# Moving the reloads of the turned queries, and the joins that follow them, through the cross-attention stage of a decoder layer

## The chip, the cores and the metric

The kernel runs on one core of a Trainium2 chip. The metric is the device time of one execution in microseconds (us); lower is better. The kernel before was run three times: 1977.21, 1982.29 and 1982.72 us, median 1982.29 us. The execution that was profiled took 1977.05 us.

## The reference

One decoder layer on 256 tokens of width 2048 in float32: two token mixers side by side (retention and a gated linear recurrence), then cross-attention over 256 memory tokens, then a gated feed-forward block, each added to the residual stream. The change lies in the cross-attention:

```python
q = (hn @ w_q).reshape(b, s, 4, 512)
k = (mem_n @ w_k).reshape(b, m, 4, 512)
v = (mem_n @ w_v).reshape(b, m, 4, 512)
logits = einsum("bshd,bmhd->bhsm", q, k) * 512 ** -0.5
p = softmax(logits, axis=-1)
o = einsum("bhsm,bmhd->bshd", p, v)
h = h + o.reshape(b, s, 2048) @ w_o
```

There are four heads of 512 columns, so head b is the b-th block of 512 columns of q, k and v, and there are four softmaxes.

## The kernel before

**Units.** Every weight matrix is streamed from HBM in pieces of 512 rows by 512 columns (1 MB, tile `raw`, six buffers, L257). ScalarE (ACT) rounds a piece to `hi` (L288) and VectorE (DVE) takes the rest, `lo` (L289); each has three buffers. TensorE (PE) multiplies the activations with both. One piece, split and multiplied, is a unit. A matrix product over two column blocks is a pair of 11 units (`PAIR_UNITS`, L105): seven of them, the q units, issue 12 matmuls, and four, the p units, issue 24. In order they are q1 p0 q3 p1 q5 q2 q6 p2 q7 q4 p3. Two of the q units use a sum of pieces that GpSimd's accumulating DMA makes (`raw` from L269), and DVE adds pieces together once more behind q5 and q6 (L294, L296).

**What orders the work.** `units` (L310) hands out the pieces. Before unit n is multiplied it splits pieces up to unit n+2 (`prefetch`, L250), and after unit n it calls what `later(m, f)` (L306) has put down for that unit; `later(m, f)` means "after m more units than the next one". So what is called after unit n stands in the program behind `hi` and `lo` of unit n+2 and ahead of those of unit n+3. A scheduler then lays the instructions of each engine into one fixed queue in the order in which a simulation finds them ready, earlier program lines first; `keep_in_program_order` holds an instruction behind everything that the program gave its engine earlier. Each engine works through its queue in order, and waits where an input is not there.

**The stage.** The units are counted here from the start of the key product: units 0 to 10 are the first key pair (heads 0 and 1), 11 to 21 the second key pair (heads 2 and 3), 22 to 32 the value pair (heads 0 and 1 of the value), and from 33 on come the single value blocks of 24 matmuls each.

The queries come out of the preceding product with tokens on the partitions. They are wanted with features on the partitions, so they are turned by DMA, which moves two-byte words only: `row_planes` (L771, copies at L760) separates the high and the low halves of the words, `KeptRows.store` (L794) puts them to HBM, `KeptRows.load` (L801) reads one head back with a transposing DMA on the queue of SyncE (SP) into a tile `d`. `join_planes` (L762) puts the halves of a pair of feature blocks together again with two copies on ACT (L766, the first of them held in program order), and `split_pair` (L551) makes the two parts for the matmul: a cast on ACT (L555) and a subtraction on DVE (L556). That chain for one pair of blocks is called a join here. Each head has one reload and two joins. The keys take the same way without HBM: `turn_key` (L1244) turns a key block by two transposing DMAs from SBUF (`turn_planes`, L777, issued at L781), calls its two joins 6 and 7 units later, and the softmax of the head 9 units later. `softmax` (L1196) issues 24 small matmuls (L521, the first held in program order), the maximum, the exponential and the division, and two units later four transposes of the probabilities on PE (L1222, the first held in program order).

| called after unit | head 0 | head 1 | head 2 | head 3 |
|---|---|---|---|---|
| reload of the query, before | 2 | 6 | 14 | 19 |
| joins of the query, before | 6, 8 | 10, 12 | 18, 20 | 23, 25 |
| turn of the key | 12 | 16 | 23 | 27 |
| joins of the key | 18, 19 | 22, 23 | 29, 30 | 33, 34 |
| softmax | 21 | 25 | 32 | 36 |

Where a join of a query and one of a key are called after the same unit, that of the query comes first, since it was put down earlier. `d`, the joined and split tiles and the block outputs share one pool of 24 tiles of 4 KB per partition (`big`).

Of the kernel before, what the change touches and what calls it, by code (L numbers as in the profile page):

```python
# [156 lines left out]
def hybrid_layer(  # L157
# [148 lines left out]
    def later(n, fn):  # L306

        pending.append((step[0] + n + 1, fn))
# [139 lines left out]
    def pair_out(w, st, ss, c0, r=None):  # L448

        o0, o1 = (big([P, 2, BW], s="o") for _ in range(2))  # L450
        if r is not None:
            neg = sp_.tile([P, 2], F32, tag="neg", name=nm("neg"))
            dve.tensor_scalar_mul(neg, r, -1.0)

        def copy(o, i, tt):
            if r is None:
                act.copy(o, i)
            else:
                act.mul(o, i, r[:, tt : tt + 1])

        def add(o, i):
            if r is None:
                dve.tensor_tensor(out=o, in0=o, in1=i, op=ALU.add)
            else:
                for tt in range(2):
                    dve.scalar_tensor_tensor(
                        out=o[:, tt, :], in0=i[:, tt, :], scalar=r[:, tt : tt + 1], in1=o[:, tt, :],
                        op0=ALU.mult, op1=ALU.add,
                    )

        def less(o, i, tt):
            if r is None:
                dve.tensor_tensor(out=o, in0=o, in1=i, op=ALU.subtract)
            else:
                dve.scalar_tensor_tensor(
                    out=o, in0=i, scalar=neg[:, tt : tt + 1], in1=o, op0=ALU.mult, op1=ALU.add
                )

        def out(kind, x, z, yu, rw):
            if kind == "q1":  # L480
                copy(o0[:, 0, :], x, 0)
            elif kind == "q5":
                for tt in range(2):
                    copy(o1[:, tt, :], z, tt)
                later(3, lambda: add(o1, rw))
            elif kind == "q6":
                less(o1[:, 0, :], x, 0)
            elif kind == "q7":
                copy(o0[:, 1, :], x, 1)
                less(o1[:, 1, :], x, 1)  # L490
            elif kind == "p3":
                add(o0, yu)

        pair_products(w, 0, st, ss, c0, c0 + BW, out)
        return o0, o1
# [748 lines left out]
    def turn_key(b, o):  # L1244
        d = turn_planes(row_planes(o))
        ks = []
        for pr in range(2):
            later(5 + pr, lambda pr=pr: ks.append(split_pair(join_planes(d, pr))))
        later(8, lambda: softmax([qs[2 * b], qs[2 * b + 1]], ks))

    for b, at in ((0, ((2, 6, 8), (6, 10, 12))), (2, ((3, 7, 9), (8, 12, 14)))):
        for i, (n, *joins) in enumerate(at):
            later(n, qs.load)
            for pr, m in enumerate(joins):
                later(m, lambda i=2 * b + 2 * i + pr: qs[i])
        for i, o in enumerate(pair_out("xa_w_k", ms, ms.sums, b * BW, rsms[0])):
            later(1 + 4 * i, lambda b=b + i, o=o: turn_key(b, o))
# [229 lines left out]
```

## Time and profile before

| | |
|---|---|
| time of the profiled execution | 1977.05 us |
| its span, first to last instruction | 1975.3 us |
| mean granted TensorE clock | 0.999 |
| ACT busy in the span | 1295.6 us (66%) |
| DVE busy in the span | 1564.9 us (79%) |
| moved by DMA | 461.29 MB, mean 234 GB/s |

Times within the profile are microseconds from the start of the span. In a row of the timeline the first two numbers are the start and the length of an instruction (or of a run of equal ones, merged, with their count at the end); then come the engine, the line, the operation, and the tile written and the tiles read; the bracket has the idle time of the engine just before and what ended it. In a row of the groups the numbers behind the bar are the busy time and the mean time of one in ns, and behind the second bar the idle time before. PE is the matmul, PEld the load of its weights, which lies beside it. SPq rows are DMAs that SP issues: the length is that of the issue, not of the transfer.

### The profile page before, as it was taken

The page shows a single profiled execution, that of the slowest core. Times are in us where ns is not written, and L with a number is a line of the kernel's source. Part 1 is how long each engine was busy: PE and PEld are TensorE (multiplying, and loading weights), DVE is VectorE, ACT ScalarE, POOL GpSimd, SP SyncE. Part 2 cuts the span into 40 slices and gives each one's busy share as a digit, 9 for nine tenths or more (in the row PEclk, how much of TensorE's full clock was granted, in tenths as well). Part 3 has the DMA queues.
Part 4 walks back from the last instruction along what each step waited for, and adds up shares of the span by engine and source line. Part 5 has one row for each costly group of instructions (what it writes and reads, how often), then busy time and mean ns, then how long its engine had stood idle before and what let it go on. Part 6 is the DMA issues. An engine that isn't in the chain of part 4 may idle for free. (4 is left out here: it accounts for less than half of the span.)

```text
span 1975.3 us, 23603 instructions
## 1 busy us (share of the span) xinstructions
PE 1961.2 (99%) x9264; PEld 1645.0 (83%) x9264; DVE 1564.9 (79%) x1546; ACT 1295.6 (66%) x1349; POOL 43.2 (2%) x52
## 2 busy tenths in 40 slices
PE   9999999999999999999999999999999999999998
PEld 8888888888888888888888888888888888888887
DVE  6988887889986886778888868777779676796775
ACT  6655656767667656667778767666765577655663
POOL 0000000000000000000000000000000000000000
PEclk9999999999999999999999999999999999999999
DMA  9675774655887776878998838867689677797671
GB/s 369 232 253 147 244 254 172 214 194 158 259 257 240 255 236 212 245 288 239 280 262 224 284 128 250 274 220 212 222 224 305 234 230 225 204 302 271 215 244 63
DMA packets 157598, 461.29 MB, mean 234 GB/s; under 512 B 88368, under 2 KB 93104, under 8 KB 109744
## 3 DMA queue, kind: packets, MB, share of 16 engines
q1 hardware_dynamic: 150208, 415.23, 60.0%
q0 software_dynamic: 5760, 41.95, 11.5%
q10 hardware_dynamic: 1520, 2.63, 0.4%
q8 instruction: 72, 1.18, 0.2%
q14 instruction: 38, 0.31, 0.0%
HBM read 422.01 MB, written 17.83 MB: 223 GB/s over the span
## 5 line engine op out<-in xcount | busy, mean ns | idle before, releaser
L289 DVE TENSOR_TENSOR lo<-raw,hi 128x2048 fp32r<-128x2048 f32 (+1 forms) x420 | 950.8, 2268 | 290.6 <-ACT hi L288 288.6
L288 ACT CAST hi<-raw 128x2048 fp32r<-128x2048 f32 (+1 forms) x418 | 792.2, 1901 | 479.7 <-PE acc L365 311.6
L364 PE MATMUL acc<-hi,s 128*128 128x512 f32 x2008 | 783.1, 390 | 0.4 <-ACT hi L288 0.2
L365 PE MATMUL acc<-hi,s 128*128 128x512 f32 x2008 | 781.6, 389 | 0.0
L371 PE MATMUL acc<-lo,s 128*128 128x512 f32 x2008 | 500.7, 389 | 0.0
L364 PEld LDWEIGHTS acc<-hi,s 128*128 128x128 f32 x2008 | 376.9, 188 | 78.4 <-ACT hi L288 0.6
L371 PEld LDWEIGHTS acc<-lo,s 128*128 128x128 f32 x2008 | 376.9, 188 | 78.3
L365 PEld LDWEIGHTS acc<-hi,s 128*128 128x128 f32 x2008 | 377.1, 188 | 77.6 <-DVE s L559 0.2
L353 PE MATMUL acc<-s,hi 128*128 128x512 f32 x832 | 201.9, 394 | 1.1 <-DVE hi L286 1.1
L353 PEld LDWEIGHTS acc<-s,hi 128*128 128x128 f32 x832 | 154.3, 189 | 31.8 <-issue 1.4
L766 ACT COPY jp<-d 128x512 uint16<-128x512 uint16 x152 | 108.4, 772 | 33.1 <-DMA d<-rp 33.1
L364 PE MATMUL acc<-hi,ss 128*128 128x512 f32 x320 | 125.9, 394 | 2.3 <-DVE nat L429 1.5
L365 PE MATMUL acc<-hi,ss 128*128 128x512 f32 x320 | 124.7, 390 | 0.0
L353 PEld LDWEIGHTS acc<-s,lo 128*128 128x128 f32 x832 | 108.0, 192 | 4.7 <-DVE lo L289 1.0
L353 PE MATMUL acc<-s,lo 128*128 128x256 f32 x832 | 111.1, 284 | 0.4 <-DVE lo L289 0.4
L371 PE MATMUL acc<-lo,ss 128*128 128x512 f32 x320 | 85.9, 390 | 0.0
L364 PEld LDWEIGHTS acc<-hi,ss 128*128 128x128 f32 x320 | 60.1, 188 | 17.4 <-DVE nat L429 3.0
L371 PEld LDWEIGHTS acc<-lo,ss 128*128 128x128 f32 x320 | 60.1, 188 | 12.6
L365 PEld LDWEIGHTS acc<-hi,ss 128*128 128x128 f32 x320 | 60.1, 188 | 12.1
L269 POOL DMA_DIRECT2D raw<-in_wall x40 | 35.2, 880 | 1555.6 <-DVE lo L289 925.1
L429 DVE TENSOR_TENSOR nat<-nat,acc 128x512 f32<-128x512 f32 (+1 forms) x49 | 44.0, 910 | 3.4 <-DMA nat<-in_x 1.7
L294 DVE TENSOR_TENSOR raw<-raw,raw 128x2048 f32<-128x2048 f32 x20 | 45.8, 2288 | 0.5
(232 smaller groups left out, 1249.1 us busy)
## 6 DMA issues: line engine op xcount, KB each, us to landing
raw<-in_wall SPq DMA_DIRECT2D x333, 1024.0 KB, 5.0
raw<-in_wall POOLq DMA_DIRECT2D x40, 1024.0 KB, 8.2
fkept<-nat SPq DMA_DIRECT2D x12, 512.0 KB, 8.0
nat<-fkept SPq DMA_DIRECT2D x12, 512.0 KB, 4.8
xt<-in_x_t SPq DMA_DIRECT2D x11, 256.0 KB, 7.8
raw<-in_wall SPq DMA_DIRECT2D x5, 512.0 KB, 8.2
nat<-in_x ACTq DMA_DIRECT2D x4, 512.0 KB, 9.8
ret<-hr SPq DMA_DIRECT2D x4, 512.0 KB, 4.8
```

Of the source, the lines that this page charges most:

```text
L269: pool.dma_start(out=raw, in_=src, accum_op=ALU.add)
L288: act.copy(hi[:, a:b], raw[:, a:b])
L289: dve.tensor_tensor(out=lo[:, a:b], in0=raw[:, a:b], in1=hi[:, a:b].bitcast(F32), op=ALU.subtract)
L294: dve.tensor_tensor(out=to, in0=to, in1=by, op=ALU.add)
L353: pe.matmul(a, part, sx, start=k == 0 and t == 0, stop=k == nk - 1 and t == 0, skip_group_check=True)
L364: pe.matmul(o, h, hi, start=start and kk == 0, stop=False, skip_group_check=True)
L365: pe.matmul(o, l, hi, start=False, stop=False, skip_group_check=True)
L371: pe.matmul(o, h, lo, start=False, stop=stop and kk == KC - 1, skip_group_check=True)
L429: dve.tensor_tensor(out=o, in0=o, in1=i, op=op)
L766: ins = act.copy(words(t)[:, :, :, 1 - i], d[:, i, 2 * pr : 2 * pr + 2, :])
```

## The change

The two lists of offsets in the loop over the key pairs are replaced. Each inner list is the unit, from the start of its key pair, after which a head's query is reloaded, and the two units after which it is joined.

```diff
-    for b, at in ((0, ((2, 6, 8), (6, 10, 12))), (2, ((3, 7, 9), (8, 12, 14)))):
+    for b, at in ((0, ((3, 14, 15), (8, 18, 19))), (2, ((8, 12, 13), (14, 19, 20)))):
         for i, (n, *joins) in enumerate(at):
             later(n, qs.load)
             for pr, m in enumerate(joins):
                 later(m, lambda i=2 * b + 2 * i + pr: qs[i])
```

In units counted from the start of the first key pair:

| | head 0 | head 1 | head 2 | head 3 |
|---|---|---|---|---|
| reload, before | 2 | 6 | 14 | 19 |
| reload, after the change | 3 | 8 | 19 | 25 |
| joins, before | 6, 8 | 10, 12 | 18, 20 | 23, 25 |
| joins, after the change | 14, 15 | 18, 19 | 23, 24 | 30, 31 |

The turns of the keys, their joins, the softmaxes and all else are called where they were.

## The prediction

> **What bounds the kernel now.** The page comes first: the span, and the busy line of its engines.
>
> ```profile
> span 1975.3 us, 23603 instructions
> PE 1961.2 (99%) x9264; PEld 1645.0 (83%) x9264; DVE 1564.9 (79%) x1546; ACT 1295.6 (66%) x1349; POOL 43.2 (2%) x52
> ```
>
> TensorE is busy for 1961.2 of 1975.3 us. All that any change of order can win is the other 14.1 us, and only the part that lies in the stretch which the change touches. So the next view is the busy time in three stretches: the first key pair (units 0 to 10), the second (11 to 21, with the softmax behind it), and the value pair (22 to 32, with two softmaxes).
>
> ```profile
> core 0: us, PE busy (x) PEld busy (x) DVE busy (x) ACT busy (x) POOL busy (x), PEclk, DMA share, GB/s
> 978.60:1019.40 40.80, 40.80 (x182) 33.80 (x181) 36.67 (x26) 32.12 (x30) 1.74 (x2) 1.00 0.96 284
> 1019.40:1063.10 43.70, 43.70 (x206) 36.70 (x205) 38.24 (x27) 35.70 (x34) 1.74 (x2) 1.00 0.97 261
> 1063.10:1111.70 48.60, 47.70 (x238) 40.16 (x237) 40.23 (x34) 40.16 (x47) 0.88 (x1) 1.00 0.81 250
> ```
>
> In both key pairs PE is busy for the whole stretch; in the value pair it lacks 0.9 us. A busy PE could still be a slow one, so the third view is PE in order of time, at the place of that gap.
>
> ```profile
> 1089.60 0.39 PE L364 MATMUL acc<-hi,ss 128*128 128x512 f32 x1
> 1089.83 0.39 PE L365 MATMUL acc<-hi,ss 128*128 128x512 f32 x1
> 1090.05 0.84 PE L371 MATMUL acc<-lo,ss 128*128 128x512 f32 x3
> 1091.80 0.30 PE L1222 MATMUL sm<-cid,prob 128*128 128x128 f32 x1 [0.90 <-DVE prob L1215]
> ```
>
> Starts lie 0.23 us apart although each row is 0.39 us long: the matmuls overlap in the array, and that is the pace throughout (182 of them in the 40.80 us of the first stretch, 0.224 us each). Three of them from 1090.05 would be followed by a fourth at 1090.73; what follows starts at 1091.80. The one stall is thus 1.07 us (0.90 us of it shows as idle time): the transposes of the probabilities of head 1 wait for DVE. By rows this is the ceiling of the gain, and the question is only what new wait arises.
>
> **The change, part by part.** Nothing is added or removed. Eight joins and four reloads are called at other units. By the places where they are called, the query joins of the first key pair go from 3 to 0, those of the second from 3 to 4, those of the value pair from 2 to 4. A join costs two copies and a cast on ACT and a subtraction on DVE:
>
> ```profile
> L766 ACT COPY jp<-d 128x512 uint16<-128x512 uint16 x28 | 20.4, 780 | 0.0
> L555 ACT CAST s<-jp 128x512 fp32r<-128x512 f32 x14 | 8.7, 619 | 0.0
> L556 DVE TENSOR_TENSOR s<-jp,s 128x512 fp32r<-128x512 f32 x14 | 9.6, 686 | 2.1 <-ACT s L555 2.0
> ```
>
> That is 2 x 0.78 + 0.62 = 2.2 us of ACT and 0.7 us of DVE. The second key pair takes one join more: ACT 35.70 + 2.2 = 37.9 of 43.70 us, DVE 38.24 + 0.7 = 38.9. The value pair takes two more: ACT 40.16 + 4.4 = 44.6 of 48.60, DVE 40.23 + 1.4 = 41.6. Both engines still fit, so the averages cost PE nothing. The first pair gains 6.6 us of ACT, which is worth nothing, since PE already runs there without a gap.
>
> Averages can hide a bunch, so the margin of a single unit is needed. This is ACT in order of time, and PE where it takes up what the second of these `hi` casts made (unit 18):
>
> ```profile
> 1034.10 1.92 ACT L288 CAST hi<-raw 128x2048 fp32r<-128x2048 f32 x1 [2.62 <-PE acc L365]
> 1035.92 0.77 ACT L766 COPY jp<-d 128x512 uint16<-128x512 uint16 x1
> 1037.77 1.92 ACT L288 CAST hi<-raw 128x2048 fp32r<-128x2048 f32 x1 [1.08 <-issue]
> ```
> ```profile
> 1043.87 0.39 PE L364 MATMUL acc<-hi,s 128*128 128x512 f32 x1
> ```
>
> The cast ends at 1039.69, 4.2 us before PE needs it, and that is with ACT running as far ahead as three buffers let it (at 1034.10 it waits for PE). Joins 0 and 1 of head 0 are now called after units 14 and 15, that is about these two casts; the idle 2.62 and 1.08 us take most of their 4.4 us. The largest bunch is after units 18, 19, 23 and 30, where a query join stands beside a key join; 18 and 23 were such places before. At 19 and 30 the addition is 2.2 us, at 24 and 31 likewise, against 4.2 us of margin. I cost all delays of `hi` and `lo` at 0. If the margin were gone, each join would cost up to 2.2 us of PE.
>
> What is left are the waits of PE for a softmax, whose matmuls keep their place in PE's queue. There are three.
>
> Softmax of head 0, after unit 21. Here are ACT and DVE ahead of it, and PE:
>
> ```profile
> 1055.27 0.61 ACT L555 CAST s<-jp 128x512 fp32r<-128x512 f32 x1
> 1055.78 0.77 ACT L766 COPY jp<-d 128x512 uint16<-128x512 uint16 x1
> 1056.42 1.90 ACT L288 CAST hi<-raw 128x2048 fp32r<-128x2048 f32 x1
> 1058.22 0.62 ACT L555 CAST s<-jp 128x512 fp32r<-128x512 f32 x1
> ```
> ```profile
> 1057.01 0.69 DVE L556 TENSOR_TENSOR s<-jp,s 128x512 fp32r<-128x512 f32 x1
> 1058.36 2.29 DVE L289 TENSOR_TENSOR lo<-raw,hi 128x2048 fp32r<-128x2048 f32 x1 [0.66 <-ACT hi L288]
> 1060.57 0.69 DVE L556 TENSOR_TENSOR s<-jp,s 128x512 fp32r<-128x512 f32 x1
> ```
> ```profile
> 1060.19 3.04 PE L521 MATMUL sm<-s,s 128*128 128x256 f32 x24
> ```
>
> By program order the join cast at 1055.27 is the key's second (called after 19), and that at 1058.22 belongs to the query of head 2 (after 20). In the changed kernel the query of head 1 joins after 19 ahead of the key, and nothing is called after 20: the key moves to the later place, and its subtraction ends at 1061.26. The 24 matmuls take 0.12 us each, and the seventh, at 1060.91, is the first to read it. Cost 0.35 us.
>
> The stall ahead of the transposes of head 1. DVE before it:
>
> ```profile
> 1085.43 0.69 DVE L556 TENSOR_TENSOR s<-jp,s 128x512 fp32r<-128x512 f32 x1
> 1086.03 0.68 DVE L1205 TENSOR_REDUCE sx<-sm 128x2 f32<-128x512 f32 x1
> ...
> 1091.29 0.62 DVE L1215 TENSOR_SCALAR prob<-prob,sx 128x256 f32<-128x256 f32 x2
> ```
>
> The subtraction at 1085.43 is that of the last join, called after 25. It goes to 31, so the chain behind it can start 0.6 us sooner; the join that comes to 24 lies earlier on DVE. Gain between 0 and 0.6 us; I take 0.3.
>
> Softmax of head 2, after unit 32: ACT, DVE and PE again.
>
> ```profile
> 1095.15 1.41 ACT L766 COPY jp<-d 128x512 uint16<-128x512 uint16 x2
> ...
> 1104.73 0.62 ACT L555 CAST s<-jp 128x512 fp32r<-128x512 f32 x1
> ```
> ```profile
> 1107.12 0.69 DVE L556 TENSOR_TENSOR s<-jp,s 128x512 fp32r<-128x512 f32 x1
> ```
> ```profile
> 1108.86 3.04 PE L521 MATMUL sm<-s,s 128*128 128x256 f32 x24
> ```
>
> The key's second part is ready at 1107.81 and first read at 1108.86 + 6 x 0.12 = 1109.58: 1.8 us of room. The query of head 3 now joins ahead of it after unit 30, 2.2 us of ACT and 0.7 of DVE if all of it falls in this chain. Cost between 0 and 2.2 + 0.7 - 1.8 = 1.1 us; I take 0.2, since ACT waits for PE once in this stretch and one of the two copies is not held in order.
>
> Sum: 0.35 - 0.3 + 0.2, about +0.2 us: 1977.3 us against the profiled execution's 1977.05 us (its span of 1975.3 us and 1.75 us around it). The runs shown have their median at 1982.29 us, 5.2 us above that execution, for a reason that the trace does not hold; the forecast on that scale is **1982.5 us**, and where the runs fall as the profiled one did, it is 1977.3.
>
> The four reloads are moved past other transfers on SP's queue. SP around the value pair, the reloads' own row, and the landing time of reloads from HBM (these four and four of another stage):
>
> ```profile
> 1081.40 7.78 SPq L781 DMA_TRANSPOSE d<-rp  x2
> 1089.27 0.53 SPq L267 DMA_DIRECT2D raw<-in_wall  x1
> ```
> ```profile
> L801 SPq DMA_TRANSPOSE d<-qs x4: 2057/5196/6581, 979.1 to 1047.8; - x4
> DMA to landing us min/median/max: 4.3/6.8/10.0
> ```
>
> The reload of head 3 leaves the second key pair, where the DMA engines are busy at 0.97, for the value pair at 0.81. Its issue holds SP for 2.1 to 6.6 us, and behind it stand the weights and the turn of a key. Called after 25, it has until 30; q5, q2, q6, p2 and q7 lie between, 4 x 12 + 24 = 72 matmuls of 0.224 us, 16.1 us, against 10.0 us for the slowest landing. I cost it at 0.
>
> The Trainium skill, DMA: Bandwidth & Descriptors, section Latency and other measured facts, gives a transposing DMA 261 GB/s, by which a head's 256 tokens of 1024 two-byte words would take an estimated 2.0 us, and a late reload could not happen. The row above speaks against it: 4.3 us at best from issue to landing, 10.0 at worst.
>
> **The rivals.** First, slower: the reload of head 3 gets in front of the turn of head 2's key on SP. For it: both want the queue at about 1081.40, the turn because it waits for its copies on ACT, and the turn holds SP for 7.78 us itself. The key planes then land up to 6.6 us later. Turns land at most 8.9 us after issue, as this row says, so the second, from about 1082.7, landed by 1091.6; it would be 1098.2, while ACT wants the first copy, which it may not pass over, at 1095.15.
>
> ```profile
> DMA to landing us min/median/max: 4.1/6.4/8.9
> ```
>
> ACT would stand for 3.0 us with the casts queued behind it, and softmax 2 would come 3.0 + 1.3 - 1.8 = 2.5 us late (1.3 for the query's two copies or copy and cast that stay in front, less the room). If the reload also waits for a free tile, as one did here for 6.1 us, it is 8.6 us:
>
> ```profile
> SPq L801 <- PE acc L365: 6.1, 1, 6.1
> ```
>
> So 1984.8 to 1990.9 us on the scale of the median. It decides from the point where the key planes land after about 1095.7. Against it: the turn is called two units earlier than this reload. Of its range only the part above 5.9 us is slower by over 0.3%.
>
> Second, a gain: the stall of 1.07 us goes whole and no softmax waits, 1981.2 us. Against it: most of the chain (an addition and a `lo` of 2.3 us each on DVE between the maximum and the division) stays.
>
> Third, the change does more than it says: the schedule of all engines is laid out anew, other tiles of the common pool are waited for, and the runs fall at the lower end of those shown, near 1977, or the fixed order costs a few us elsewhere. Nothing in the trace bears on its sign. The unused 14.1 us of PE bound the gain.
>
> **How the numbers follow.** The forecast, within 2 us of either 1977.3 or 1982.5 us, has 0.60; the first rival 0.20 (half of it under 5.9 us); joins that the margins of 4.2 us do not cover, at 2.2 us each and three or more of them, 0.05; the gain 0.05; the new layout 0.10, evenly to both signs. Two measurements of this kernel can't be told apart below about 0.3%, 5.9 us. Faster by more than that needs 42% of all idle time of PE: 0.05, from the third rival alone. Slower by more: 0.10 from the first, 0.05 from the margins and 0.05 from the third: 0.20. The rest, 0.75, is within 0.3%. The range runs from 1976.0, the lower level less the whole stall, to 1990.0, nearly the end of the first rival; the forecast's own is 1977 to 1984.
>
> **What would show it.** Right: PE busy within 1 us of the stretch in all three stretches, no `hi` or `lo` waited for, waits only in front of L521 and L1222 and under 1 us each; the first key pair with 6 us less of ACT. Wrong: a copy at L766 that waits for DMA with PE idle behind it (first rival), a PE wait for L288 or L289 in units 14 to 20 (the margins), or idle time of PE outside units 0 to 40 (third rival).

## The result and the profile after

| | before | after |
|---|---|---|
| median | 1977.64 us (20 runs, 1975.06 to 1991.26) | 1984.11 us (20 runs, 1980.53 to 2000.67) |
| time of the profiled execution | 1977.05 us | 1983.62 us |
| runs above 1985 us | 1 of 20 | 9 of 20 |

The ratio is 1.0035, with a 95% interval from 1.0019 to 1.0051: the changed kernel is slower by 6.5 us. Two of the three runs of before that were known at first lay high (median 1982.29); with 17 more the median is 1977.64, where the profiled execution was. Both profiled executions stand close to their medians, so the traces can be compared.

The page of the changed kernel, its span and the busy line of TensorE:

```profile
span 1981.8 us, 23607 instructions
PE 1963.0 (99%) x9264; PEld 1645.6 (83%) x9264; DVE 1564.3 (79%) x1546; ACT 1295.2 (65%) x1349; POOL 43.2 (2%) x52
```

The span grew by 6.5 us and PE's busy time by 1.8, so 4.7 us are new idle time. The three stretches of the stage, with their borders set by the same matmuls as before (0.6 to 0.7 us earlier, the last 0.2 later):

```profile
978.00:1018.70 40.70, 40.70 (x182) 33.68 (x181) 34.36 (x22) 27.40 (x21) 1.74 (x2) 1.00 0.98 282
1018.70:1062.40 43.70, 43.66 (x203) 36.44 (x202) 36.95 (x25) 36.85 (x37) 1.75 (x2) 1.00 0.93 249
1062.40:1111.90 49.50, 48.31 (x235) 39.79 (x234) 38.03 (x35) 41.02 (x51) 0.87 (x1) 1.00 0.91 223
```

ACT's busy time shows the joins leaving the first pair (32.12 us became 27.40). PE idles for 0.04 us in the second stretch and 1.2 in the third, against 0.9 before: up to here nearly nothing is lost. The loss stands behind the stretch. PE's waits from 978 to 1160 us in the changed kernel (total, times, longest):

```profile
PE sm L521 <- ACT v L570: 3.6, 1, 3.6
PE acc L364 <- ACT o L457: 0.8, 1, 0.8
PE sm L521 <- DVE s L556: 0.3, 1, 0.3
```

The last of them stands in the softmax of head 2. The softmax of head 0 has no wait; its 24 matmuls only take 3.33 us, where they took 3.04 before:

```profile
1059.49 3.33 PE L521 MATMUL sm<-s,s 128*128 128x256 f32 x24
...
1110.43 2.30 PE L521 MATMUL sm<-s,s 128*128 128x256 f32 x17 [0.34 <-DVE s L556]
```

The first of the waits is the product of the probabilities with the value of head 0 (`attend`), which waits for a copy on ACT (L570). PE in order of time at that place, and then busy time and clock (the third number from the end) in two stretches there:

```profile
1125.30 0.40 PE L364 MATMUL acc<-hi,s 128*128 128x512 f32 x1
1129.25 1.22 PE L521 MATMUL sm<-ps,v 128*128 128x256 f32 x4 [3.56 <-ACT v L570]
1130.27 0.63 PE L365 MATMUL acc<-hi,s 128*128 128x512 f32 x1
1130.70 0.63 PE L364 MATMUL acc<-hi,s 128*128 128x512 f32 x1
```
```profile
1125.30:1129.20 3.90, 0.40 (x2) 0.00 (x0) 3.39 (x5) 3.90 (x7) 0.00 (x0) 0.83 0.58 218
1129.20:1134.80 5.60, 5.55 (x20) 4.97 (x21) 2.54 (x3) 0.62 (x1) 0.00 (x0) 0.51 0.61 225
```

Behind the 3.56 us of idle time the matmuls start 0.43 us apart instead of 0.23, and the granted clock is 0.51 for 5.6 us. That loses another 5.6 x 0.49 = 2.7 us by estimate, which counts as busy time of PE. 3.6 + 2.7 = 6.3 us: nearly the whole loss is at one place. The Trainium skill, TensorE: Matmul & The Clock Gate, Part 1, says that an idle window of some 3.4 us brings the clock to half; the trace agrees with that here (3.56 us idle, then 0.51).

Why is that copy late? ACT back to the start of the delay:

```profile
1089.03 2.02 ACT L760 COPY rp<-o 128x1024 uint16<-128x1024 uint16 x2
1095.37 1.91 ACT L288 CAST hi<-raw 128x2048 fp32r<-128x2048 f32 x1 [4.32 <-DMA raw<-in_wall]
...
1119.22 0.56 ACT L1210 ACTIVATE prob<-sm,sx,lscale 128x256 f32<-128x256 f32 x1 [4.82 <-DVE sx L1206]
...
1128.00 0.58 ACT L1230 COPY pT<-sm 128x512 f32<-128x512 f32 x1
1128.47 1.34 ACT L570 ACTIVATE v<-o,ro 128x512 fp32r<-128x512 f32 x2
```

Read it from below. The copy at 1128.47 comes at the end of nine us in which ACT had no gap, and these began with the exponential of softmax 2 at 1119.22, which ACT had waited for. DVE took its maximum 5.8 us later than in the kernel before (first row after, second before):

```profile
1118.24 0.68 DVE L1205 TENSOR_REDUCE sx<-sm 128x2 f32<-128x512 f32 x1
```
```profile
1112.40 0.69 DVE L1205 TENSOR_REDUCE sx<-sm 128x2 f32<-128x512 f32 x1
```

In front of that stands a row of casts and joins that was pushed back by the 4.32 us at 1091.05, in which ACT waited for the weights of unit 30. Those weights are the sum of two pieces that GpSimd's accumulating DMA makes. Here are its issue and SP's queue, in the changed kernel:

```profile
1080.96 0.87 POOL L269 DMA_DIRECT2D raw<-in_wall  x1 [19.81 <-DVE raw L296]
```
```profile
1078.12 2.62 SPq L781 DMA_TRANSPOSE d<-rp  x2
1080.83 1.80 SPq L801 DMA_TRANSPOSE d<-qs  x1
```

And the DMAs issued in this stretch with their time to landing, first of the changed kernel, then of the kernel before:

```profile
raw<-in_wall POOLq DMA_DIRECT2D x1, 1024.0 KB, 14.3
...
d<-qs SPq DMA_TRANSPOSE x1, 15.1
```
```profile
raw<-in_wall POOLq DMA_DIRECT2D x1, 1024.0 KB, 8.4
```

The reload of head 3 goes out 0.13 us ahead of the accumulating DMA. Both land after 14 to 15 us, where the accumulating DMA took 8.4 before and no reload of the stage over 10.0. The accumulating DMA itself was issued at the same time in both kernels (1080.96 and 1080.99): it is slower, not later.

**Theory.** The loss is this meeting: a transposing reload that comes ahead of an accumulating DMA. The accumulating DMA lands late, ACT loses 4 us, and ACT's backlog reaches PE some 34 us later, behind the softmax of head 2. **Rivals.** The bunched joins alone fill ACT's time in the value pair; or the data of head 3 come late, and what needs them waits. The experiments move the reload, move the joins, and put in reloads that nothing reads.

### The profile page after: what moved, and what is told of

Read it like the earlier page. It is cut to its first block, busy times and chain, and to the rows that moved or that the text cites. A ratio compares the mean times of both kernels' runs of the same rounds, so it can differ in the third digit from the quotient of the medians.

```text
span 1981.8 us, 23607 instructions
## 1 busy us (share of the span) xinstructions
PE 1963.0 (99%) x9264; PEld 1645.6 (83%) x9264; DVE 1564.3 (79%) x1546; ACT 1295.2 (65%) x1349; POOL 43.2 (2%) x52
## 3 DMA queue, kind: packets, MB, share of 16 engines
q0 software_dynamic: 5760, 41.95, 11.7%
## 5 line engine op out<-in xcount | busy, mean ns | idle before, releaser
L288 ACT CAST hi<-raw 128x2048 fp32r<-128x2048 f32 (+1 forms) x418 | 791.9, 1900 | 488.5 <-PE acc L365 316.2
L364 PE MATMUL acc<-hi,s 128*128 128x512 f32 x2008 | 783.6, 390 | 0.0
L364 PEld LDWEIGHTS acc<-hi,s 128*128 128x128 f32 x2008 | 377.4, 188 | 77.6 <-ACT s L558 0.3
L766 ACT COPY jp<-d 128x512 uint16<-128x512 uint16 x152 | 108.0, 770 | 33.7 <-DMA d<-rp 33.5
L364 PE MATMUL acc<-hi,ss 128*128 128x512 f32 x320 | 126.2, 394 | 3.6 <-DVE nat L429 1.9
L364 PEld LDWEIGHTS acc<-hi,ss 128*128 128x128 f32 x320 | 60.1, 188 | 19.4 <-DVE nat L429 3.2
```

What stands on the lines that cost most here:

```text
L288: act.copy(hi[:, a:b], raw[:, a:b])
L364: pe.matmul(o, h, hi, start=start and kk == 0, stop=False, skip_group_check=True)
L766: ins = act.copy(words(t)[:, :, :, 1 - i], d[:, i, 2 * pr : 2 * pr + 2, :])
```

## The experiments

All were run in five rounds beside the kernel before on the same chip (17 to 35 runs of it, 11 or 12 of each kernel); the list of offsets is the only line that differs, unless a diff shows more. The ratio is estimated on its own and can differ from that of the two medians (e7: 1.0026, where the medians give 1.0008). Of the 116 runs of the kernel before in these rounds 8 lie above 1985 us, 5 of them beside e5 to e8 (35 runs).

| kernel | median | before | ratio, 95% interval | runs above 1985 |
|---|---|---|---|---|
| e1 reloads of heads 2, 3 back | 1981.31 | 1977.83 | 1.0022 [1.0002, 1.0041] | 3 of 12 |
| e2 before, head 3 as changed | 1980.34 | 1977.83 | 1.0025 [1.0004, 1.0045] | 4 of 12 |
| e3 reload of head 3 after 22 | 1979.35 | 1977.83 | 1.0021 [1.0001, 1.0040] | 3 of 12 |
| e4 before + unused reload after 25 | 1978.30 | 1977.83 | 1.0003 [0.9989, 1.0016] | 1 of 12 |
| e5 before, heads 0, 1 as changed | 1979.92 | 1978.42 | 1.0021 [0.9992, 1.0051] | 3 of 12 |
| e6 `attend` one unit later | 1980.46 | 1978.42 | 1.0013 [0.9994, 1.0031] | 2 of 12 |
| e7 reload of head 3 after 28 | 1979.96 | 1978.42 | 1.0026 [0.9999, 1.0053] | 4 of 12 |
| e8 as e3 + unused reload after 25 | 1979.03 | 1978.42 | 1.0009 [0.9992, 1.0027] | 1 of 12 |
| e9 all reloads at their old units | 1978.48 | 1976.96 | 1.0003 [0.9993, 1.0012] | 0 of 11 |
| e10 as e3 + unused reload after 24 | 1979.57 | 1976.96 | 1.0013 [0.9999, 1.0027] | 2 of 12 |
| e11 before + unused reload after 8 | 1988.63 | 1976.96 | 1.0050 [1.0028, 1.0071] | 9 of 12 |
| e12 both reloads behind the adds | 1978.14 | 1978.06 | 1.0003 [0.9993, 1.0013] | 0 of 12 |

Below, "add" is the accumulating DMA of GpSimd.

### Moving the reload of head 3 (e1, e2, e3, e7)

e1, the changed kernel with the reloads of heads 2 and 3 at 14 and 19:

```diff
-(2, ((8, 12, 13), (14, 19, 20)))
+(2, ((3, 12, 13), (8, 19, 20)))
```

> The changed kernel with the reloads of heads 2 and 3 called after units 14 and 19 again, as before the change; all joins stay where the change put them. Theory A (the reload of head 3 meets the accumulating DMA of the second weight sum in the value pair, 1080.8 us in the changed kernel, and the weights come 6 us late): the wait of ACT's weight cast for DMA in the value pair falls from 4.3 us to under 1, the wait of PE for the split of the values (L521 for L570) from 3.6 us to under 0.5, TensorE stays at its full clock there, and the time is within 0.1% of the kernel before, about 1 us above it at most. Theory B (the joins themselves, two more of them after units 30 and 31, crowd ACT and DVE in front of the third softmax and the first product with the values): the wait for L570 stays at 3 us or more and the time stays 0.2 to 0.4% above the kernel before.

e2, the kernel before with the reload of head 3 at 25 and its joins at 30 and 31:

```diff
-(2, ((3, 7, 9), (8, 12, 14)))
+(2, ((3, 7, 9), (14, 19, 20)))
```

> The kernel before with head 3 alone moved: its reload from unit 19 to 25, its joins from 23 and 25 to 30 and 31. Theory A: the loss is all here; ACT waits 3 us or more for the weights in the value pair, PE 3 us or more for L570, and the time is 0.25 to 0.45% above the kernel before. If the loss comes from the joins of heads 0 to 2 or from the new layout of the queues, this kernel stands within 0.1% of the kernel before. Theory B expects the same loss as theory A here; the two part in the other three runs.

e3, the changed kernel with the reload of head 3 at 22, three units earlier:

```diff
-(2, ((8, 12, 13), (14, 19, 20)))
+(2, ((8, 12, 13), (11, 19, 20)))
```

> The changed kernel with the reload of head 3 called after unit 22 in place of 25; all joins stay. The reload then goes out ahead of the turn of head 2's key and of the accumulating DMA, some 6 to 10 us sooner. Theory A: the accumulating DMA lands within 10 us of its issue (14.3 us in the changed kernel), ACT waits for weights under 1.5 us, the wait of PE for L570 goes, and the time is within 0.1% of the kernel before. Theory B: nothing changes against the changed kernel, 0.3% above the kernel before.

e7, the changed kernel with that reload at 28, so late that it stands behind the turn of head 3's key:

```diff
-(2, ((8, 12, 13), (14, 19, 20)))
+(2, ((8, 12, 13), (17, 19, 20)))
```

> The changed kernel with the reload of head 3 called after unit 28 in place of 25, which puts it behind the turn of head 3's key on SP, about 10 us after the issue of the accumulating DMA; all joins stay. Theory A (it is the meeting of the two transfers that costs): the accumulating DMA lands in 8 to 10 us, ACT does not wait for weights above 1 us there, and the time falls by 2 us or more against the changed kernel, unless the join after 30, which now finds its reload only just landed, holds ACT; then ACT shows a wait for d of 1 to 6 us with no wait for weights. Theory C (any reload in the value pair costs, whenever it goes out): the time stays 0.3% above the kernel before with ACT waiting for weights.

Where the reload isn't issued right ahead of the add of the value pair, the 3.6 us go. The waits of PE from 978 to 1160 us in e1 and e7 (e3 has the last two rows of e7 and no other):

```profile
PE acc L364 <- ACT o L457: 0.7, 1, 0.7
PE sm L521 <- ACT v L570: 0.7, 1, 0.7
PE sm L521 <- DVE s L556: 0.5, 1, 0.5
```
```profile
PE acc L364 <- DVE o L475: 15.8, 1, 15.8
PE acc L364 <- ACT o L457: 0.8, 1, 0.8
PE sm L521 <- ACT v L570: 0.7, 1, 0.7
```

The wait for `v` is 0.7 us in all three, with the joins as in the changed kernel; the add took 8.3, 8.3 and 8.4 us. So the joins alone do not make it. In e7 the reload comes latest of all, and no copy waits for it (ACT's one wait for `d` in this stage, 0.9 us at 991.36, is for head 0): late data of head 3 do not make it either.

The joins have a share in it, though. From the start of softmax 0 to the maximum of softmax 2 it takes 52.2 us in the kernel before, 54.9 in e3, which has the joins of the changed kernel and no meeting, and 58.8 in the changed kernel: 2.7 us of the delay come with the joins and 3.8 with the meeting. The joins use up room of which PE then misses 0.7 us; what the meeting adds finds none left. No run has this meeting with the joins of the kernel before, so its price there is not known.

e1 did not come down as far as was expected: its median lies 3.5 us above the kernel before, where 1 us was the most allowed for, and three of its runs took 1988.8 us and more. In its profile the stage has 1.9 us of waits, the first three rows above, and no add of the stage took over 9.5 us; another 2.4 us of waiting stand ahead of the stage, for a `hi` (L288). Where its other runs lost their time is not known; its reload of head 1 goes out 3.9 us ahead of an add, of which more below.

In e2 the joins of the other heads are those of before, and the meeting is there again, 0.14 us apart. Its DMAs in the stretch:

```profile
raw<-in_wall POOLq DMA_DIRECT2D x1, 1024.0 KB, 18.6
...
d<-qs SPq DMA_TRANSPOSE x1, 19.4
```

Its runs spread: five from 1976.4 to 1978.7 us, two at 1979.5 and 1981.2, five from 1984.6 to 1999.1; so the meeting probably doesn't come about in every run, or doesn't cost the same in each. The profiled one (span 1997.0) had it, and a second one at 1236 us.

What was not expected is the 15.8 us of PE in e7. It is in the first key pair and has the same cause with another reload, that of head 1. SP, POOL and the landing times there:

```profile
991.49 7.01 SPq L801 DMA_TRANSPOSE d<-qs  x1
```
```profile
994.82 0.87 POOL L269 DMA_DIRECT2D raw<-in_wall  x1 [16.21 <-DVE raw L296]
```
```profile
raw<-in_wall POOLq DMA_DIRECT2D x1, 1024.0 KB, 26.0
...
d<-qs SPq DMA_TRANSPOSE x1, 26.6
```

The change had moved this reload too. It is called two units later (8 for 6) and yet goes out 12 us earlier. Here are SP and POOL of the kernel before, then of the changed kernel:

```profile
1000.36 4.36 SPq L801 DMA_TRANSPOSE d<-qs  x1
```
```profile
993.04 0.88 POOL L269 DMA_DIRECT2D raw<-in_wall  x1 [17.48 <-DVE raw L296]
```
```profile
988.45 4.52 SPq L801 DMA_TRANSPOSE d<-qs  x1
```
```profile
992.33 0.88 POOL L269 DMA_DIRECT2D raw<-in_wall  x1 [17.49 <-DVE raw L296]
```

Before, it came 7.3 us behind the add; now it comes 3.9 us ahead. The add took 22 to 26 us in two of the profiles with this order (e7, e10: 3.3 and 3.5 us ahead) and 8.9 to 11.2 us in the other seven, all 3.9 us ahead. It is a second risk that the change brings, in part of the executions.

### Where PE pays (e6)

The product with the values of heads 0 and 1 is called one unit later. This kernel puts the blocks of the attention output down in another order, so the product behind it multiplies blocks of other heads; the amount of work is the same.

```diff
-        later(1 + 3 * i, lambda b=i, o=o: attend(b, split_rows(o, rsms[0])))
+        later(2 + 3 * i, lambda b=i, o=o: attend(b, split_rows(o, rsms[0])))
```

> The changed kernel with the products of the probabilities and the values of heads 0 and 1 called one unit later (36 and 39 in place of 35 and 38 by the count of units already multiplied). Theory A: the collision of the reload and the accumulating DMA stays (14 us or more to landing, ACT waits 4 us or more for weights), but what PE pays for it, the wait in front of the first product with the values and the half clock behind it, goes: no wait of PE for L570 above 0.5 us, the clock full, and the time 3 us or more under the changed kernel. If PE pays elsewhere (the weights themselves come too late for PE), the time stays at the changed kernel's.

The add takes 14.3 us and the reload 15.1 as in the changed kernel, and ACT waits its 4.3 us. The two longest of PE's waits:

```profile
PE sm L521 <- DVE v L571: 1.4, 1, 1.4
PE acc L364 <- ACT o L457: 0.8, 1, 0.8
```

With one unit more of room 1.4 us are left of the 3.6, and no long idle time follows; the median is 3.7 us under the changed kernel's, across two batches. The meeting is the cause; the place where PE was short of room sets the price.

### Reloads that nothing reads (e4, e8, e10, e11)

The same function was added in all four, at one place each:

```diff
+    def spare_reload():
+        d = big([P, 2, KC, S], U16, s="d")
+        sp.dma_start_transpose(out=d.rearrange("p a c s -> p (a c) s"), in_=qs.rows[0])
...
+        if b == 2:
+            later(14, spare_reload)
```

e4 puts it behind unit 25 of the kernel before; e8 behind 25 and e10 behind 24 (`later(13, ...)`) of e3; e11 behind unit 8 of the kernel before (`if b == 0`, `later(8, ...)`).

> The kernel before with one reload more, called after unit 25 into a tile that nothing reads; all joins and the four reloads stay where they were. Theory A: the accumulating DMA of the second sum in the value pair (8.4 us to landing before) takes 12 us or more, ACT waits 2 us or more for weights there, and the time rises by 0.1 to 0.35%; if only ACT's backlog were harmless without the later joins, the wait of ACT is there and the time rises less than 0.1%. Theory B: a transfer that nothing waits for costs nothing, under 0.05%, and no wait for weights appears.

> The changed kernel with the reload of head 3 after unit 22 (as in the third of the first runs, 0.08% above the kernel before), and a spare reload after unit 25 into a tile that nothing reads, where the changed kernel has the real one. Theory A: the spare goes out within 1 us ahead of the accumulating DMA, which lands in 12 us or more; ACT waits 3 us or more for weights, PE for L570, and the time is 3 us or more above that of the kernel without the spare, though no instruction waits for it. Theory D (the cost is that the joins of head 3 wait for a late reload): the spare costs nothing, under 1 us.

> The changed kernel with the reload of head 3 after unit 22, and a reload that nothing reads after unit 24, to come right behind the turn of head 2's key as the reload of head 3 does in the changed kernel. If the order of the two transfers makes the loss, it shows when the unused reload is issued within 1 us ahead of the accumulating transfer of unit 30: that one lands in 14 us or more, the `hi` behind it waits 4 us or more, and the time comes 3 to 5 us above that of the kernel with the reload at 22 alone (1979.35 us, 1.0 to 1.5 us above the kernel before). If the loss comes from the late data of head 3 itself, nothing reads this reload and the time stays within 1 us of that kernel. Where the unused reload comes behind the accumulating transfer, both expect no loss.

> The kernel before with a reload that nothing reads after unit 8, where the changed kernel has the reload of head 1, that is 3 to 4 us ahead of the accumulating transfer of the first key pair. If such a transfer is hurt in only part of the executions (in one profile of eight it took 26 us there, in the others 9.4 to 11.2), most runs stay within 1 us of the kernel before and a few come 10 to 20 us above, more of them than with the kernel before; the profile has the accumulating transfer at 9 to 12 us, or at 20 us or more with a wait of PE in the first key pair of over 10 us. If the late joins of head 1 were what made those runs slow, no run moves.

In e4, e8 and e10 the spare reload came behind the add of the value pair, by 8.4, 1.9 and 1.6 us, and PE shows no wait for it at that place. So they do not put the first case to the test that they were made for, but they show the other order. SP, POOL and the landing times of e8:

```profile
1084.15 6.44 SPq L1253 DMA_TRANSPOSE d<-qs  x1
```
```profile
1082.28 0.88 POOL L269 DMA_DIRECT2D raw<-in_wall  x1 [19.81 <-DVE raw L296]
```
```profile
raw<-in_wall POOLq DMA_DIRECT2D x1, 1024.0 KB, 8.5
...
d<-qs SPq DMA_TRANSPOSE x1, 8.5
```

Behind the add, the reload's own issue takes 6.44 us and the add lands in 8.5 us, as without it.

The profiled run of e4 is one of its long ones (1984.52 us) and loses its time elsewhere, ahead of the spare reload. ACT stands for the reload of head 2, and PE waits 4.8 us for a block that ACT empties behind it (L459):

```profile
1042.20 0.76 ACT L766 COPY jp<-d 128x512 uint16<-128x512 uint16 x1 [5.49 <-DMA d<-qs]
```

Up to the spare reload this kernel has the same order on ACT, DVE and SP as the kernel before, so this is a way in which that kernel too can have a long run: a copy at L766 that waits for a reload, as the first rival had it, with another head. The reload went out 1.0 us ahead of an add, and they took 7.8 and 9.8 us. The changed kernel joins head 2 later (23 and 24 for 18 and 20).

e11 settles it. ACT and DVE run the same instructions in the same order as in the kernel before. The spare reload went out at 1012.33, 2.2 us ahead of the first add of the second key pair (1014.49). Landing times, and PE's waits from 978 to 1160:

```profile
raw<-in_wall POOLq DMA_DIRECT2D x1, 1024.0 KB, 25.0
...
d<-qs SPq DMA_TRANSPOSE x1, 24.5
```
```profile
PE acc L364 <- ACT hi L288: 6.7, 1, 6.7
PE acc L364 <- ACT o L459: 2.2, 1, 2.2
```

Nothing reads this transfer, no join and no other reload was moved, and the median is 11.7 us above the kernel before; 11 of 12 runs lie at 1984 to 2003 us, and one, at 1975.33, is as fast as any run of before. It was expected in the first key pair and in few runs; the profile has it in the second, and nearly all runs are long. ACT's longest wait, 13.6 us, ends within 0.1 us of the landing of the add. Two other things happen beside it. The two weight pieces that SP issues during the meeting, plain transfers of 1 MB, take 18.6 and 19.0 us; in e7 and e10 such pieces took 17.0 to 22.0, where the middle one of the stage takes 5.9 to 6.9 in every profile, and the longest without a meeting 16.1 (e4). And the issue of the spare reload holds SP for 10.0 us, so that the next piece goes out at 1022.43 instead of 1017.81. What share of the 11.7 us each has was not separated. What the DMA engines did between 1012 and 1034 us (last two columns: their busy share, GB/s), in e11 and in the kernel before:

```profile
1012.00:1034.00 22.00, 22.00 (x99) 18.23 (x98) 12.64 (x10) 12.77 (x14) 0.86 (x1) 1.00 1.25 131
```
```profile
1012.00:1034.00 22.00, 22.00 (x99) 18.23 (x98) 18.36 (x14) 17.62 (x18) 0.86 (x1) 1.00 0.92 275
```

They are not idle by this count; they move half the bytes in the same time. That speaks for transfers that hinder one another, not for a lack of work, but it does not show how.

### The joins alone (e5, e9)

e5 is the kernel before with heads 0 and 1 as changed; e9 is the changed kernel with all reloads called at 2, 6, 14 and 19.

```diff
-for b, at in ((0, ((2, 6, 8), (6, 10, 12))), (2, ((3, 7, 9), (8, 12, 14)))):
+for b, at in ((0, ((3, 14, 15), (8, 18, 19))), (2, ((3, 7, 9), (8, 12, 14)))):
```

> The kernel before with heads 0 and 1 alone moved (reloads 3 and 8, joins 14, 15, 18, 19). The first runs left 1.7 to 1.9 us that PE loses in this stage without any collision. Theory A1: that part lies in front of the first softmax, where the key's second join now stands behind a query join (0.2 to 0.5 us), and in the value pair, where the joins of head 3 are; so this kernel shows a wait of PE for L556 under 0.6 us at the first softmax, no wait for weights, and stands within 0.05% of the kernel before. Theory A2: the part comes from the joins of heads 0 and 1 in the second key pair (ACT and DVE late for units 14 to 20); then PE loses 1.5 us or more before 1063 us and the time is 0.08% or more above.

```diff
-for b, at in ((0, ((3, 14, 15), (8, 18, 19))), (2, ((8, 12, 13), (14, 19, 20)))):
+for b, at in ((0, ((2, 14, 15), (6, 18, 19))), (2, ((3, 12, 13), (8, 19, 20)))):
```

> The changed kernel's joins, with all four reloads at the units of the kernel before (2, 6, 14, 19). If the loss has two parts, joins (about 1.5 to 2 us, found with part of the reloads still moved) and a reload that meets an accumulating transfer (4 to 5 us), this kernel keeps the first alone: 1.5 to 2 us above the kernel before, the accumulating transfer of the value pair lands in 8 to 9 us, no `hi` of the value pair waits for weights for over 1 us, PE waits under 1 us for the value of head 0. If the joins' part was really that of the reloads which had stayed moved in the earlier runs (heads 0 and 1), it is within 0.5 us of the kernel before. If bunched joins alone make the loss, it stays 5 to 7 us above.

In e5 seven joins meet in the second key pair, more than in either kernel, and PE waits 2.2 us for `hi` of unit 21; so joins can cost something once ACT has no gap left. That is a mixture of both kernels and not a part of the change. Its reload of head 1, too, goes out 3.9 us ahead of the add, and 3 of its 12 runs are long. e9 is 1.5 us above the kernel before by the medians, with an interval that holds no change, and its runs keep together (1977.53 to 1980.32). In its profile the key's second part comes late for the softmax of head 0, and PE waits 1.9 us there, the wait that the prediction sized at 0.35. It is not quite "joins alone": the reload of head 1, though called at 6, goes out 3.9 us ahead of its add here too, since the scheduler gives it that place as soon as the joins are late. Its add took 8.9 us in the profile, and none of the 11 runs was long.

### The change without the meetings (e12)

The changed kernel with the reload of head 3 after 28 and that of head 1 after 12; all joins stay where the change put them.

```diff
-for b, at in ((0, ((3, 14, 15), (8, 18, 19))), (2, ((8, 12, 13), (14, 19, 20)))):
+for b, at in ((0, ((3, 14, 15), (12, 18, 19))), (2, ((8, 12, 13), (17, 19, 20)))):
```

> The changed kernel with the reload of head 3 after unit 28, behind the accumulating transfer of the value pair, and that of head 1 after unit 12, behind the accumulating transfer at 992 us instead of 3.9 us ahead of it. If the loss is joins plus reloads that come ahead of accumulating transfers, the joins' 1.5 us stay (1978.3 to 1979.5 us median), no accumulating transfer of units 0 to 32 takes over 10 us, and runs above 1985 us become as rare as with the kernel before. The new place of head 1's reload may come ahead of the next accumulating transfer at 1032 us: if it does, by under 4 us, long runs can remain. If the bunched joins made the long runs, the spread stays that of the changed kernel.

```profile
PE acc L364 <- ACT o L457: 0.8, 1, 0.8
PE sm L521 <- ACT v L570: 0.7, 1, 0.7
```

1978.14 us against 1978.06: the loss is gone, and so are the long runs (11 of 12 lie from 1977.81 to 1980.34), though on this chip the kernel before had none above 1985 us either (0 of 17). The reload of head 1 went out 2.9 us behind the add at 1014.29. The two waits that the joins leave are worth 1.5 us, for the 0.9 us before the transposes that the change took away; the medians differ by 0.1 us, the lower quarters by 1.7 (1977.9 against 1976.2). So the joins cost between 0 and about 1.7 us, and the two reloads, by difference, the rest of the 6.5. The 12 kernels gave no version that beats the kernel before.

## How far the prediction was right, step by step

The forecast was 1982.5 us and no change beyond 0.3%, with a range from 1976.0 to 1990.0. 1984.1 was measured, inside the range. That is luck: 1982.5 was built on the median of three runs, two of them high, and with 20 runs the kernel before has its median at 1977.64. The forecast difference was +0.2 us, the measured one is +6.5, in the direction and about the size of the case "slower by over 0.3%", which had 0.20 (the interval of the ratio, 1.0019 to 1.0051, holds the bound of 0.3%). The step that failed is the one on the reloads.

- **What bounds the kernel: right.** PE does, and nearly all of the loss is PE waiting or at half clock at one place.
- **Joins at 0: nearly right.** No `hi` or `lo` was late for a join, and e12 shows that all eight joins in their new places cost 0 to 1.7 us. The first key pair gave up 4.7 us of ACT, not 6.6. But the prediction asked only whether ACT gives weights in time. ACT also empties PE's accumulators (L457): there PE waits 0.8 us, since that copy, at 1088.09, now stands behind the exponential of head 1 at 1086.99, and before it stood ahead of it.
- **Softmax 0, +0.35: right in the changed kernel**, 0.3 us in the length of its 24 matmuls. It is not firm: with the same joins it was 0.5 us of waiting in e1 and 1.9 in e9.
- **Transposes, -0.3 within 0 to -0.6: the wait went altogether**, 0.9 us of idle time, since DVE's chain came free; 0.8 us came back at L457, as said. The net was about nothing.
- **Softmax 2, +0.2 within 0 to 1.1: the size is inside, the reason is another.** PE waits 0.34 us there, and by the start of its matmuls the stage fell back by 0.6 us. But in e3, e7 and e12, with the same joins and no such meeting here, there is no wait in this softmax, and in e6, with the meeting, there is the same 0.34: it comes from ACT's 4.3 us for the weights.
- **Reloads at 0: this step failed**, and with it the forecast. The prediction compared the reload's own landing with the unit that needs it (16.1 us of time against 10.0 of landing). The reload landed in 15.1 us and was in fact in time. The harm was done to a neighbour: the accumulating DMA on POOL's queue, issued 0.13 us later. The text named SP's queue and the raw pieces in it, and never looked at what POOL issues beside it; POOL's row of 40 accumulating DMAs was on the page. And the place of the reload of head 1 was read from the unit after which it is called, while the schedule put it out 12 us earlier.
- **First rival: right about which transfer, wrong about its victim.** It named the reload of head 3 near 1081 us and priced it at 2.5 to 8.6 us by way of the key's turn; the loss of 6.5 us lies within that by chance. The turn went ahead of the reload, as the text held against it. The turn's copies came in time; the weights of unit 30 did not.
- **The signs.** None of the three signs of being wrong came: no copy at L766 waited for a DMA in front of a loss, no weights were late in units 14 to 20, and nearly all of the new idle time lies in the stage. What failed were signs of being right: PE idles 1.2 us in the value pair, where 1 was the most, and of the waits, which were to stay under 1 us at L521 and L1222, one at L521 has 3.6 us and one of 0.8 us is at L364. No sign named the path that the loss took, a weight cast (L288) that waits for an accumulating DMA.
- **What the prediction left out:** behind 3.6 us of waiting PE runs 5.6 us at a clock of 0.51, so such a wait costs 2.7 us more than itself.

**What stays open.** Why a transposing DMA and an accumulating DMA slow one another when the first is ahead and not when it is behind, and when they do. The distance alone does not decide. It came in each of three profiles at 0.13 to 0.14 us ahead (changed kernel, e2, e6) and in e11 at 2.2 us. But reloads of head 2 stand 1.0 to 3.3 us ahead of an add without it: 1.0 us in e4 (the add took 9.8), 1.7 in e9 (9.9), 2.1 in e1 (8.4), 3.2 in the kernel before (7.9). With the reload of head 1, 3.3 to 3.9 us ahead, it came in two profiles of nine; with turns of another stage, 0.6 to 0.7 us ahead of an add near 1230 us, in two (e2, e3: 22 us), while the others there took 8.8 to 9.7 us. One thing goes with part of it: in e7, e10 and e11, and in e2 and e3 near 1230 us, a plain transfer issued ahead of the pair was in flight for 3 to 5 us more after the add was issued. In the harmless cases there was none, or it landed within about 1 us; e6 is an exception (3.3 us, and that add took 11.2). At 0.13 to 0.14 us there was no such transfer. So it may be a cause or an effect, and it is not the only one; it was not tried. Of the long runs of the kernel before, the profile of e4 shows one way; whether others come from meetings like these is not known.

## What to carry to other kernels

When a DMA is moved, lay all queues side by side at its new place, those of other engines included, and ask who is in flight just behind it: here the transfer that moved was in time, and its neighbour was not. In the longest meetings the plain loads behind them were late too. Read the new place from the schedule that results, not from the line that calls it. And a spread of runs that grows (9 of 20 above 1985 us, where it was 1 of 20) is a finding of its own: look in a profile of a long run for the one transfer that took three times as long.

## What the runs showed of the hardware

- A reload of 512 KB with transposition ahead of an accumulating DMA of 1 MB: 14.3 to 26.0 us for the latter in six profiles (changed kernel, e2, e6, e7, e10, e11), and 15.1 to 26.6 us for the reload. All other adds of the stage, in all profiles, took 7.8 to 12.9 us. With the reload behind the add, the add took 7.8 us (the kernel before, head 1), 8.5 (e8) and 8.8 (e12). The issue of the reload then took 4.4, 6.4 and 7.6 us, but 6.6 us also in the kernel before with no add in flight (1047.82).
- During such a meeting (e11, 1012 to 1034 us) the DMA engines count as fully busy and move 131 GB/s; without it they moved 275 in the same stretch. Plain loads of 1 MB issued meanwhile took 17.0 to 22.0 us (e7, e10, e11); the medians of the stage lie at 5.9 to 6.9.
- TensorE idle for 3.56 us: granted clock 0.51 for the next 5.6 us, matmuls 0.43 us apart instead of 0.23.
